# A hybrid layer with a 32-expert MoE: the first expert's up products move into the output-projection stage

## The chip, the cores and the metric

The kernel runs on one core of a Trainium2 chip. The metric is device time in microseconds (us) for one execution. Inputs lie in device memory at the start and the output lies there at the end. The names of the engines are those of the profile: PE is the matrix engine, DVE the vector engine, ACT the scalar engine, POOL the GpSimd engine, and SP the engine that here only issues transfers.

## What is computed

One layer on 2048 tokens of width 1024, in float32: a norm, an input projection, a mixer of 4 mLSTM heads and 4 differential-attention heads, an output projection with a residual, and then the part that matters here, a mixture of experts (MoE) with a residual:

```python
def hierarchical_moe(h, w_group, b_group, w_expert, b_expert, w_gate, w_up, w_down):
    ...
    g_logits = (xt @ w_group).astype(f32) + b_group.astype(f32)
    g_sel = jnp.argmax(g_logits, axis=-1)
    ...
    top_vals, top_idx = lax.top_k(e_in, TOP_K)            # 2 of the 8 experts of one of 4 groups
    eid = (g_sel[:, None] * EXPERTS_PER_GROUP + top_idx).reshape(-1)
    ...
    def expert_block(args):
        xb, e = args
        hid = jax.nn.silu(xb @ w_gate[e]) * (xb @ w_up[e])  # 1024 -> 512, twice
        return hid @ w_down[e]                              # 512 -> 1024
    ...
        h = rms_norm(x, norm2_w[l])
        x = x + hierarchical_moe(h, w_group[l], b_group[l], w_expert[l], b_expert[l],
                                 w_gate[l], w_up[l], w_down[l])
```

So each token goes to two of 32 experts, chosen by its own normalised row, and the experts' token counts depend on the data.

## The kernel before

**Stages.** The input projection and the mixer fill the first half of the span. Then the output projection runs over 16 blocks of 128 tokens (lines 886 to 1162). For each block it multiplies with w_out, adds the residual (`add_half`, line 956), computes the norm's scale (`finish_half`), writes the normalised rows to `h2_d` (`normed`), turns them for the router (`turn_x2`, line 986), computes the router's logits (line 1007 to 1018), and picks experts (`route_a`, `route_b`). `route_b` works out a slot in the table `tb_d` for each token and choice (2048 slots for each expert, filled in token order from `base`), scatters token numbers and weights there by two indirect transfers on POOL's queue (line 1077), and adds to the counts `cnt`. Block i's routing is issued within the loop of block i+1, so only block 15's lies bare at the end.

**Ranking.** After block 15, lines 1136 to 1162 rank the experts by their counts and write `cnti`: which expert stands at which of 32 places, and its count. Experts 0 and 1 are FIXED at places 0 and 1. PE, DVE, ACT and POOL each load their place's count from `cnti` into a register (line 1331) before they go on with a place, and SP loads the expert numbers.

**MoE.** Lines 1163 to 1413 run over the places in an order of instructions written by hand. Each engine runs its instructions in this order. Every weight is split in a high and a low part of a reduced float32 type, and each product takes three matmuls (high by high, low by high, high by low). `ready(u)` splits half a weight tile: the high part on ACT (line 66), the low part on DVE (line 70). Raw weights lie in a ring of 12 slots `R4`, an expert has 6 (4 for gate and up, 2 for down), split tiles lie in a ring of 4, and splits run LOOK = 6 halves ahead of the products. `done(e, j)` reloads a raw slot with the weights of two places on. A place gathers its first 128 tokens' rows from `h2_d` into `xg`, turns them (line 1204), makes 48 up matmuls (`ffn1`, line 1231), the gated hidden layer (`hidden`, lines 1211 to 1213), turns that (`turn_h`, line 1236), and makes 24 down matmuls (`ffn2`, line 1246) one place later, within the next place's turn.

**Later tokens.** If a place has more than 128 tokens, a branch `more{e}` also runs the "few" path: it turns 32 or 64 further rows (line 1265), multiplies them with the raw weights in plain float32 (up at line 1276, down at line 1291), and scatters the result. It reads the same raw slots, which come free for the next weights only behind it.

**The seam** below is the stretch from block 15's routing to the first expert's products. The first six splits stand there, at lines 1319 and 1320, behind the ranking.

## Time and profile before

| what | value |
|---|---|
| median of 3 runs | 2172.4 us (2168.9 to 2178.18) |
| the profiled execution | 2168.61 us, of which the span is 2166.9 us |
| mean granted PE clock in it | 0.981 |
| PE busy | 2048.8 us, 95% of the span |
| DVE, ACT, POOL busy | 1603.8, 1230.9 and 517.1 us |
| projection stage with ranking, about | 1150 to 1378 us |
| MoE, about | 1378 to 2155 us |

The span runs from the first to the last instruction of the profiled execution. The granted clock is a share of full speed, which is 2.4 GHz. A busy share is an average over stages that have different limits, so the rows further down are all from the seam and from the first places of the MoE.

### The profile page before, as it was taken

What the parts mean: (1) busy time and instruction counts of PE and PEld (TensorE: products, weight loads), DVE (VectorE), ACT (ScalarE), POOL (GpSimd) and SP (SyncE); (2) the same over time, 40 slices, a digit from 0 to 9 for tenths busy, and PEclk for the clock granted to TensorE, in tenths of its full rate; (3) what the DMA queues carried; (4) which work ended last, traced back from release to release, by engine and by line L of the source; (5) the groups of instructions that cost most, each with busy time, mean ns of one, the idle gap of its engine ahead of it and who ended that gap; (6) DMA issues with size and microseconds to landing.
All of it is one profiled execution on the core that took longest, in us unless ns stands there. A gap on an engine that the chain in (4) does not pass through costs nothing. (4 is left out here: it accounts for less than half of the span.)

```text
span 2166.9 us, 40488 instructions
## 1 busy us (share of the span) xinstructions
PE 2048.8 (95%) x13815; PEld 1735.3 (80%) x13816; DVE 1603.8 (74%) x4373; ACT 1230.9 (57%) x2820; POOL 517.1 (24%) x685
## 2 busy tenths in 40 slices
PE   7999998999999999999999999599999999999997
PEld 6888887899899999999987888477777666766865
DVE  7667655887788778878886777787887656776863
ACT  5334334666566566656663333477777656667764
POOL 4000004323322332232201111213232332213322
PEclk9999998999999999999999999799999999999999
DMA  7555439645653646375417854499999768898983
GB/s 232 180 171 182 150 111 243 181 123 131 186 152 110 173 149 156 89 195 162 122 51 256 270 145 136 153 328 331 360 344 334 263 218 295 309 317 285 345 285 80
DMA packets 241526, 449.79 MB, mean 208 GB/s; under 512 B 36368, under 2 KB 120400, under 8 KB 231248
## 3 DMA queue, kind: packets, MB, share of 16 engines
q1 hardware_dynamic: 192160, 316.56, 43.3%
q0 software_dynamic: 48800, 128.46, 22.1%
q8 instruction: 161, 2.64, 0.5%
q14 instruction: 133, 1.09, 0.1%
q10 hardware_dynamic: 272, 1.05, 0.1%
HBM read 378.51 MB, written 84.25 MB: 214 GB/s over the span
## 5 line engine op out<-in xcount | busy, mean ns | idle before, releaser
L70 DVE TENSOR_TENSOR L<-R,H 128x1024 fp32r<-128x1024 f32 x408 | 485.9, 1223 | 122.7 <-ACT H L66 119.0
L66 ACT ACTIVATE H<-R 128x1024 fp32r<-128x1024 f32 x408 | 415.8, 1056 | 27.8 <-DVE cnti L1158 9.2
L1231 PE MATMUL pgu<-H,xT 128*128 128x512 f32 x1024 | 360.1, 410 | 14.4 <-issue 5.9
L1231 PEld LDWEIGHTS pgu<-H,xT 128*128 128x128 f32 x1024 | 196.1, 192 | 57.5 <-issue 15.7
L585 ACT ACTIVATE prob<-sc,nm 128x512 f32<-128x512 f32 (+3 forms) x320 | 195.9, 623 | 48.9 <-DVE nm L582 44.0
L574 DVE TENSOR_REDUCE mx<-sc 128x1 f32<-128x512 f32 (+3 forms) x320 | 186.9, 602 | 32.4 <-PE sc L573 16.5
L1231 PE MATMUL pgu<-L,xT 128*128 128x512 f32 x512 | 203.0, 397 | 0.0
L570 PE MATMUL sc<-kt,qt 128*128 128x512 f32 (+3 forms) x640 | 190.2, 387 | 10.1 <-DMA kt<-k_d 7.8
L1246 PE MATMUL py<-H,hT 128*128 128x512 f32 x512 | 177.2, 409 | 11.8 <-issue 10.2
L629 PE MATMUL w<-va,aT 128*128 128x128 f32 x1088 | 155.7, 277 | 6.0 <-ACT raw L510 4.4
L94 PE MATMUL w<-H,hs 128*128 128x256 f32 x512 | 156.6, 306 | 5.0 <-DVE num L690 4.4
L500 PE MATMUL w<-hs,H 128*128 128x256 f32 x512 | 157.8, 308 | 2.0 <-ACT tho L545 0.9
L474 POOL DMA_DIRECT2D qt<-q_d x128 | 77.9, 615 | 296.7 <-DMA q_d<-qkT 274.6
L629 PEld LDWEIGHTS w<-va,aT 128*128 128x128 f32 x1088 | 139.3, 191 | 11.6 <-ACT raw L510 7.3
L95 PE MATMUL w<-L,hs 128*128 128x256 f32 x512 | 145.8, 285 | 0.0
L96 PE MATMUL w<-H,hs 128*128 128x256 f32 x512 | 145.5, 284 | 0.0
L502 PE MATMUL w<-hs,L 128*128 128x256 f32 x512 | 144.8, 283 | 0.0
L501 PE MATMUL w<-hs,H 128*128 128x256 f32 x512 | 144.7, 283 | 0.0
L1246 PEld LDWEIGHTS py<-H,hT 128*128 128x128 f32 x512 | 98.2, 192 | 45.1 <-issue 23.1
L570 PEld LDWEIGHTS sc<-kt,qt 128*128 128x128 f32 x640 | 100.5, 192 | 18.1 <-issue 7.9
L1193 POOL DMA_INDIRECT xg<-h_d,ix x64 | 90.4, 1412 | 97.6 <-PE pt L1204 35.7
L1308 POOL TENSOR_SCALAR yE<-yE,ix 32x1024 f32<-32x1024 f32 (+1 forms) x20 | 57.0, 2852 | 232.0 <-ACT yE L1307 223.9
(374 smaller groups left out, 5227.7 us busy)
## 6 DMA issues: line engine op xcount, KB each, us to landing
R<-w_gate SPq DMA_DIRECT2D x128, 512.0 KB, 10.9
R<-w_up SPq DMA_DIRECT2D x128, 512.0 KB, 11.8
R<-w_down SPq DMA_DIRECT2D x63, 1024.0 KB, 12.7
hs<-hT_d POOLq DMA_DIRECT2D x62, 1024.0 KB, 5.3
hT_d<-hs SPq DMA_DIRECT2D x16, 1024.0 KB, 3.9
qt<-q_d POOLq DMA_DIRECT2D x128, 128.0 KB, 6.4
xt<-x SPq DMA_DIRECT2D x30, 512.0 KB, 4.7
q_d<-qkT SPq DMA_DIRECT2D x32, 256.0 KB, 3.3
```

What stands on the lines that cost most here:

```text
L66: return A.activation(dst, src, AF.Copy, scale=scale)
L70: return V.tensor_tensor(dst, src, h.bitcast(F32), OP.subtract)
L94: T.matmul(ps, xh, wh, start=start, stop=False)
L95: T.matmul(ps, xh, wl, start=False, stop=False)
L96: T.matmul(ps, xl, wh, start=False, stop=stop)
L500: T.matmul(ps, l0, m0, start=d == 0, stop=False)
L570: T.matmul(ps[:, :n], QT[g // 2][:, o, m, g % 2 * P:(g % 2 + 1) * P], KT[r * 4 + c][:, m, :n], start=o == 0, stop=o == 1 and c < sb)
L574: V.reduce_max(B["mx"][:, m, c:c + 1], ps[:, :n], axis=AX.X)
L585: mark["ACT"] = A.activation(B["p", m][:, c2 * 512:c2 * 512 + n], B["sc", m, c2][:, :n], AF.Exp, bias=nm, scale=0.125, accum_out=B["rs"][: ...
L629: T.matmul(po, B["aT", c][:, kb * P:(kb + 1) * P], VA[r * 4 + c][:, kb, :], start=c == 0 and kb == 0, stop=c == nch - 1 and kb == nb[c] - 1)
L1231: T.matmul(pgu[c], xT[:, l, d, :], r[:, :, n], start=d == 0 and m == 0, stop=d == DC - 1 and m == 2)
L1246: T.matmul(py[n], hT[:, l, f, :], r[:, c], start=f == 0 and m == 0, stop=f == 3 and m == 2)
```

## The change

It has three parts. **Early slots.** In block 15's loop, `first_slots` raises `base` and `cnt` of expert 0 to at least 128, so that its tokens of the last two blocks go to slots from 128 on, loads the slots that blocks 0 to 13 filled (`ix0`), and gathers their rows to `xg1`. Expert 0 has 96 tokens with the reference's inputs (worked out from its router); 85 of them are in blocks 0 to 13 and 11 in the last two, so its count becomes 139, and the branch `more0` is taken, which it wasn't. **Early products.** The six first splits, the turn of `xg1` (`first_turn`) and 48 up matmuls (`first_up`) with eight more splits and the gated hidden layer now stand in the projection stage; the last six splits are held behind `posi`, the slots of block 15. In the MoE, place 0 has no up products: it turns `TH`, makes its 24 down matmuls at once, then turns place 1's rows and runs its few path; place 1 has no down products beside its up products. **Room.** For this, four tiles moved to an earlier pool, one weight slot fewer is loaded early (EARLY, 11 to 10), the router's weights lie in a raw slot, and block 15's `normed` runs in one pass on DVE rather than on ACT and POOL.

```diff
-EARLY = 11
+EARLY = 10
...
+        xg1 = wp.tile([P, D], F32, name="xg1")
+        xTs = [wp.tile([P, 2, DC, P], F32R, name="xT0")]
+        TH = [wp.tile([P, 256], F32, name=f"TH{c}") for c in range(2)]
+        ix0 = wp.tile([P, 2, 4], F32, name="ix0")
+
...
-            if e:
-                order_of_use += [6 * (e - 1) + 4, 6 * (e - 1) + 5]
+            if e != 1:
+
+                f = max(e - 1, 0)
+                order_of_use += [6 * f + 4, 6 * f + 5]
 
         def first_half(e):
 
-            return 12 * e - 4 if e else 0
+
+            return 12 * e - 4 if e > 1 else 12 * e
...
                 rows = slice(i * P, (i + 1) * P)
-                CT[i] = sp.tile([P, D], F32, name="ct", bufs=1)
...
-            wr = sp.tile([P, DC, NL], F32, name="wr", bufs=1)
+            wr = R4[9][:, :DC * NL].rearrange("p (c n) -> p c n", c=DC)
...
                 R = RT[i]
-                if i < NB - 1:
-                    V.scalar_tensor_tensor(R["h2"], XT[i], R["ry"], n2b, op0=OP.mult, op1=OP.mult)
-                else:
-                    A.activation(R["h2"], XT[i], AF.Copy, scale=R["ry"])
-                    G.tensor_tensor(R["h2"], R["h2"], n2b, OP.mult)
+                V.scalar_tensor_tensor(R["h2"], XT[i], R["ry"], n2b, op0=OP.mult, op1=OP.mult)
                 nc.sync.dma_start(h2_d[i * P:(i + 1) * P, :], R["h2"])
...
                 posi = sp.tile([P, 2], I32, name="posi")
-                V.tensor_copy(posi, pos)
+                mark["DVE"] = V.tensor_copy(posi, pos)
                 st = [G.indirect_dma_start(out=tb_d, out_offset=bass.IndirectOffsetOnAxis(ap=posi[:, j:j + 1], axis=0),
                                            in_=en[:, j, :], in_offset=None) for j in range(2)]
                 tc.declare_no_dep(st[1].ins, st[0].ins, reason="slots of another expert")
                 V.tensor_tensor(cnt, pr[:, 1, :], cnt, OP.add)
+
+            def first_slots():
+
+                V.tensor_scalar(base[:, 0:1], base[:, 0:1], float(P), None, op0=OP.max)
+                V.tensor_scalar(cnt[:, 0:1], cnt[:, 0:1], float(P), None, op0=OP.max)
+                nc.sync.dma_start(ix0[:, 0], tb_d[0:P, :])
+                G.indirect_dma_start(out=xg1, out_offset=None, in_=h2_d[:S - 2 * P],
+                                     in_offset=bass.IndirectOffsetOnAxis(ap=ix0[:, 0, 0:1].bitcast(I32), axis=0),
+                                     bounds_check=S - 2 * P - 1, oob_is_err=False)
+
+            def first_turn(hf):
+                pt = pp.tile([P, 4, P], F32, name="pt", bufs=2)
+                for j in range(4):
+                    T.transpose(pt[:, j, :], xg1[:, (hf * 4 + j) * P:(hf * 4 + j + 1) * P], ident)
+                h = slice(hf * 4, hf * 4 + 4)
+                split_h(xTs[0][:, 0, h, :], pt)
+                split_l(xTs[0][:, 1, h, :], pt, xTs[0][:, 0, h, :])
+
+            def first_up(pgu, d):
+                wh, wl = (t.rearrange("p (m n) -> p m n", m=2) for t in parts(d // 2, d % 2))
+                for c in range(2):
+                    n = slice(c * 256, (c + 1) * 256)
+                    for m, (l, r) in enumerate(((0, wh), (0, wl), (1, wh))):
+                        T.matmul(pgu[c], xTs[0][:, l, d, :], r[:, :, n], start=d == 0 and m == 0, stop=d == DC - 1 and m == 2)
+
+            def gated(th, pgu, n, behind=None):
+                a1 = A.activation(th, pgu[:, :n], AF.Tanh, scale=0.5)
+                v1 = V.scalar_tensor_tensor(th, th, 1.0, pgu[:, :n], op0=OP.add, op1=OP.mult)
+                if behind:
+
+                    after(a1, behind["ACT"])
+                    after(v1, behind["DVE"])
+                V.tensor_tensor(th, pgu[:, n:2 * n], th, OP.mult)
+                return th
 
             finish_block(0, None)
...
                         route_b(i - 2)
+                    if i == NB - 1 and d == 1:
+                        first_slots()
                     if i + 1 < NB and d in (4, 6):
                         turn_block(i + 1, d // 2 - 2)
...
                 part(d, 1)
+                if d < LOOK:
+                    ready(d)
                 if d == 0:
                     route_b(i - 1)
+                if d in (2, 3):
+                    first_turn(d - 2)
                 if d == 4:
                     turn_x2(i, 0)
...
             route_a(i)
+            route_b(i)
             normed(i)
-            route_b(i)
+            pgu = [pp.tile([P, 512], F32, name=f"pj{n}", bufs=2) for n in range(2)]
+            for d in range(DC):
+                first_up(pgu, d)
+                sl = ready(d + LOOK)
+                if d + LOOK >= DC:
+                    after(sl, mark["DVE"])
+            for c in range(2):
+                gated(TH[c], pgu[c], 256, mark)
...
                 tc.tile_pool(name="pm", bufs=1, space=PSUM, reuse_waits="tile") as pp:
             R4 += [sp.tile([P, 2048], F32, name=f"R{j}", bufs=1) for j in range(EARLY, RAWS)]
             xg0 = sp.tile([P, D], F32, name="xg0", bufs=1)
-            xg1 = sp.tile([P, D], F32, name="xg1", bufs=1)
             yE = sp.tile([P, D], F32, name="yE", bufs=1)
-            for t in (xg0, xg1, yE):
+            xTs.append(sp.tile([P, 2, DC, P], F32R, name="xT1", bufs=1))
+            for t in (xg0, yE):
                 G.memset(t, 0.0)
 
...
                                                 max_val=NE - 1, skip_runtime_bounds_check_because="a place's expert")
+                    if i == 0:
+                        IX[0] = ix0
+                        nc.sync.dma_start(ix0[:, 1], tb_d[P:2 * P, :])
+                        return
 
                     IX[i] = sp.tile([P, 2, 4], F32, name="ix2", bufs=AHEAD + 5)
                     e = eid[i]
...
             why = "counts of 2048 tokens"
-            for i in range(AHEAD):
+            for i in (1, 0, 2):
                 fetch_slots(i)
-            gather(IX[0][:, 0], xg1)
             gather(IX[1][:, 0], xg0)
-            for u in range(LOOK):
-                ready(u)
-            xT = new_xT()
-            turn(xT, xg1)
 
             for t in range(EARLY, RAWS):
                 load_next(t, nc.scalar)
-            py, hT, th, waiting = None, None, None, None
+            xT, py, hT, th, waiting = None, None, None, TH, None
             for e in range(NE + 1):
                 u = first_half(e)
                 fetch_slots(e + AHEAD)
                 if e < NE:
                     n = nc.values_load(cnti[:1, n_at + e:n_at + e + 1], min_val=0, max_val=S, skip_runtime_bounds_check_because=why)
                     gather(IX[e][:, 1], xg1)
-                    xTn = new_xT() if e + 1 < NE else None
-                    pgu = new_pgu()
+                    xTn = new_xT(e + 1) if e + 1 < NE else None
+                    if e:
+                        pgu = new_pgu()
+                    else:
+
+                        hT, py = new_hT(), new_py()
+                        for d in range(2):
+                            turn_h(TH[d], hT, d)
+                        for f in range(4):
+                            ffn2(py, hT, f, parts(4 + f // 2, f % 2))
+                            ready(8 + f + LOOK)
                     for d in range(DC):
-                        ffn1(pgu, xT, d, parts((u + d) // 2, d % 2))
-                        ready(u + d + LOOK)
-                        if d < 2 and e:
+                        if e:
+                            ffn1(pgu, xT, d, parts((u + d) // 2, d % 2))
+                            ready(u + d + LOOK)
+                        if d < 2 and e > 1:
                             if d == 0:
                                 hT = new_hT()
                             turn_h(th[d], hT, d)
...
                             tc.mark_branch_hint_location(f"more{e}", n > P, engines)
-                    thn = [hidden(p, 256) for p in pgu]
+                    thn = [gated(TH[c], pgu[c], 256) for c in range(2)] if e else TH
                 else:
                     emit(*waiting)
                     hT = new_hT()
                     for d in range(2):
                         turn_h(th[d], hT, d)
                     thn = None
-                if e:
+                if e > 1:
...
                 def down(f):
-                    if e:
+                    if e > 1:
                         v = first_half(e) + (8 if e < NE else 0) + f
                         ffn2(py, hT, f, parts(v // 2, v % 2))
...
-                if e:
-                    waiting = (py, IX[e - 1][:, 0])
+                waiting = None if e == 1 else (py, IX[max(e - 1, 0)][:, 0])
                 if e < NE:
                     xT, th = xTn, thn
```

**How the rows stand.** Three places show it. The lists are of DVE's and PE's instructions in program order; `L` and `H` are the split tiles, `R` a raw slot, `TH` the hidden layer of place 0, `pt` and `pj` and `py` PSUM tiles, and + stands for the change, - for before (the line numbers are each kernel's own).

DVE, second half of block 15, one piece of the difference:

```order
+L1080 CAST posi<-pos 128x2
 L70 TENSOR_TENSOR hT<-pt,hT 128x4x128
-L956 TENSOR_TENSOR xt<-pj_17792,xt 128x512
-L978 TENSOR_TENSOR ss<-ss 128x1
+L70 TENSOR_TENSOR L_3616<-R_15365,H_3615 128x1024
+L964 TENSOR_TENSOR xt<-pj_17779,xt 128x512
+L1072 MEMSET en 128x2
+L70 TENSOR_TENSOR L_3618<-R_15366,H_3617 128x1024 x2
+L986 TENSOR_TENSOR ss<-ss 128x1
```

Splits (`L` from `R` and `H`) now stand among block 15's own work, ahead of the residual addition of its second half (L964, before L956) and of the norm's scale.

DVE at the end of the stage, before:

```order
-L1147 TENSOR_SCALAR o_18066<-ident,oc 32x32
-L1154 TENSOR_REDUCE oc<-t_18057 32x1
-L1150 TENSOR_SCALAR o_18066<-prk,oc 32x32
-L1151 TENSOR_REDUCE oc<-o_18066 32x1
-L1152 TENSOR_SCALAR o_18066<-io_15396,oc 32x32
-L1158 CAST cnti<-prk 1x64
-L70 TENSOR_TENSOR L_115<-R_112,H_113 128x1024 x2
-L70 TENSOR_TENSOR L_116<-R_15364,H_114 128x1024 x2
-L70 TENSOR_TENSOR L_3616<-R_15365,H_3615 128x1024 x2
-L70 TENSOR_TENSOR xT<-pt,xT 128x512 x2
```

and in the change:

```order
+L1189 SCALAR_TENSOR_TENSOR t_18147<-cnt,m_15402 32x96
+L1080 CAST posi<-pos 128x2
+L70 TENSOR_TENSOR L_115<-R_15367,H_113 128x1024 x2
+L70 TENSOR_TENSOR L_116<-R_15368,H_114 128x1024 x2
+L70 TENSOR_TENSOR L_3616<-R_15369,H_3615 128x1024 x2
+L1112 SCALAR_TENSOR_TENSOR TH_15375<-TH_15375,pj_18075 128x256
+L1112 SCALAR_TENSOR_TENSOR TH_15376<-TH_15376,pj_18076 128x256
+L1117 TENSOR_TENSOR TH_15375<-pj_18075,TH_15375 128x256
+L1117 TENSOR_TENSOR TH_15376<-pj_18076,TH_15376 128x256
+L1191 TENSOR_REDUCE oc<-t_18147 32x3
```

Six splits and the four gating operations, which were behind the ranking or not there, now stand between `posi` and the rest of the ranking.

PE at the end of the stage and the begin of the MoE, before:

```order
-L1149 MATMUL prk<-o_18066,ones_15410 32x32
-L1156 MATMUL prk<-o_18066,pcol 1x32
-L1157 MATMUL prk<-o_18066,oc 1x32
-L1204 MATMUL pt<-ident,xg_18096 128x128 x8
-L1331 TENSOR_LOAD cnti
-L1231 MATMUL pgu<-H_113,xT 128x512
-L1231 MATMUL pgu<-L_115,xT 128x512
```

and in the change, the same place:

```order
+L1201 MATMUL prk<-o_18156,ones_15412 32x32
+L1208 MATMUL prk<-o_18156,pcol 1x32
+L1209 MATMUL prk<-o_18156,oc 1x32
+L1378 TENSOR_LOAD cnti
+L1288 MATMUL pt<-ident,TH_15375 128x128 x2
+L1288 MATMUL pt<-ident,TH_15376 128x128 x2
+L1298 MATMUL py_18221<-H_113,hT 128x512
+L1298 MATMUL py_18221<-L_115,hT 128x512
```

and, 20 matmuls further on, from the last two down matmuls of place 0 to the first raw up matmuls of its few path:

```order
+L1298 MATMUL py_18222<-L_116,hT 128x512
+L1298 MATMUL py_18222<-H_114,hT 128x512
+L1260 MATMUL pt<-ident,xg_18186 128x128 x4
+L1408 REGISTER_ALU
+L1517 BRANCH_PREFETCH_HINT
+L1260 MATMUL pt<-ident,xg_18186 128x128 x4
+L1427 COMPARE_AND_BRANCH
+L1428 REGISTER_ALU
+L1517 BRANCH_PREFETCH_HINT
+L1317 MATMUL pt<-ident,xg_15373 128x32 x8
+L1328 MATMUL px<-R_112,xH 32x256 x8
```

The up products of place 0 that followed the load of `cnti` are gone from there; behind the load come the hidden layer's turn, the 24 down matmuls, the turn of place 1's rows, a branch, and the few path (L1317, L1328).

## Rows read from the trace of the kernel before

**Rows 1.** The page: each engine's busy time, share of the span, instructions.

```profile
PE 2048.8 (95%) x13815; PEld 1735.3 (80%) x13816; DVE 1603.8 (74%) x4373; ACT 1230.9 (57%) x2820; POOL 517.1 (24%) x685
```

**Rows 2.** Windows of the seam: length, engines' busy time (instructions), PEclk, DMA share, GB/s.

```profile
1353.96:1377.62 23.66, 9.73 (x52) 6.84 (x50) 18.85 (x89) 5.20 (x14) 8.70 (x10) 0.73 0.18 68
...
1385.02:1401.36 16.34, 13.96 (x57) 10.69 (x57) 13.65 (x16) 11.41 (x14) 3.63 (x3) 0.88 0.94 336
...
1386.00:1388.00 2.00, 1.78 (x5) 1.27 (x5) 1.64 (x3) 1.73 (x2) 0.68 (x1) 0.50 1.00 347
...
1401.36:1415.47 14.11, 14.11 (x60) 11.28 (x61) 10.89 (x13) 8.67 (x12) 1.41 (x2) 0.88 0.29 81
...
1402.00:1406.00 4.00, 4.00 (x13) 3.06 (x12) 2.32 (x3) 1.33 (x2) 0.00 (x0) 0.57 0.01 0
```

**Rows 3.** Waits of DVE from 1353.96 to 1377.62: total, times, longest.

```profile
DVE xt L956 <- PE pj L96: 1.3, 1, 1.3
DVE ss L978 <- ACT h L976: 0.8, 1, 0.8
...
DVE hT L70 <- ACT hT L66: 0.5, 1, 0.5
```

**Rows 4.** Timeline of DVE at the seam: start, length, line, operation.

```profile
1368.19 1.48 DVE L1036 CAST sel<-xe 128x2 f32<-128x2 uint32 x1
...
1373.30 0.37 DVE L1147 TENSOR_SCALAR o<-ident,oc 32x32 f32<-32x32 f32 x1
...
1374.55 2.31 DVE L1152 TENSOR_SCALAR o<-io,oc 32x32 f32<-32x32 f32 x1
...
1377.41 0.21 DVE L1158 CAST cnti<-prk 1x64 int32<-1x64 f32 x1 [0.55 <-PE prk L1157]
...
1378.84 6.96 DVE L70 TENSOR_TENSOR L<-R,H 128x1024 fp32r<-128x1024 f32 x6 [1.22 <-ACT H L66]
...
1385.73 1.27 DVE L70 TENSOR_TENSOR xT<-pt,xT 128x512 fp32r<-128x512 f32 x2
...
1416.78 0.41 DVE L1212 SCALAR_TENSOR_TENSOR th<-th,pgu 128x256 f32<-128x256 f32 x1
```

**Rows 5.** Timelines of POOL, SP and PE at the seam.

```profile
1374.97 1.86 POOL L1174 MEMSET xg<- 128x1024 f32 x2
...
1380.24 1.92 POOL L1193 DMA_INDIRECT xg<-h_d,ix  x1 [0.30 <-DVE L L70]
...
1378.35 0.40 SPq L1189 DMA_DIRECT2D ix<-tb_d  x1
...
1383.20 1.94 PE L1204 MATMUL pt<-ident,xg 128*128 128x128 f32 x8 [5.82 <-DMA xg<-h_d,ix]
```

**Rows 6.** Windows of down products, a few path, and an undisturbed expert's up products.

```profile
1415.47:1420.91 5.44, 5.44 (x25) 4.50 (x24) 5.37 (x9) 5.20 (x7) 1.00 (x1) 1.00 0.98 383
...
1451.11:1463.36 12.25, 12.25 (x131) 8.09 (x131) 7.11 (x11) 5.70 (x13) 0.00 (x0) 1.00 0.84 302
...
1463.36:1475.71 12.35, 12.35 (x61) 10.14 (x60) 10.90 (x12) 11.79 (x17) 6.56 (x4) 1.00 1.03 355
```

**Rows 7.** Timelines of PE, ACT and DVE in the first few path.

```profile
1453.31 3.66 PE L1276 MATMUL px<-R,xH 128*32 128x256 f32 x64
...
1458.39 0.27 PE L1282 MATMUL pt<-ident,th 128*128 128x128 f32 x1
...
1459.98 1.93 PE L1291 MATMUL px<-R,hH 128*32 128x256 f32 x32
...
1451.58 0.53 ACT L1267 ACTIVATE xH<-pt 128x128 f32<-128x128 f32 x2
...
1458.70 0.28 ACT L1283 ACTIVATE hH<-pt 128x128 f32<-128x128 f32 x1 [0.34 <-PE pt L1282]
...
1457.66 0.29 DVE L1213 TENSOR_TENSOR th<-px,th 128x128 f32<-128x128 f32 x1
```

**Rows 8.** Waits of PE from 1353 to 1452.

```profile
PE pgu L1231 <- DVE th L1213: 2.2, 1, 2.2
```

More of the change, by code (lines that the diff above doesn't have):

```diff
@@ L874, in split @@
             split_h(hi, raw)
-            split_l(lo, raw, hi)
+            return split_l(lo, raw, hi)
         def ready(u):
             if u < 2 * len(order_of_use):
-                split(order_of_use[u // 2] % RAWS, u // 2, u % 2)
+                return split(order_of_use[u // 2] % RAWS, u // 2, u % 2)
         def done(e, j):
@@ L941, in block_kernel @@
             before = sp.tile([P, P], BF16, name="before", bufs=1)
-            jp = sp.tile([P, P], I32, name="jp", bufs=1)
+            jp = R4[9][:, 512:512 + P].bitcast(I32)
             G.iota(jp, pattern=[[1, P]], base=0, channel_multiplier=-1)
@@ L1195, in gather, with new_xT @@
                                      bounds_check=S - 1, oob_is_err=False)
-            def new_xT():
-                return sp.tile([P, 2, DC, P], F32R, name="xT")
+            def new_xT(i=0):
+                return xTs[i % 2]
             def turn(xT, xg, hfs=(0, 1)):
@@ L1207, in turn, with hidden @@
                     split_l(xT[:, 1, h, :], pt, xT[:, 0, h, :])
-            def hidden(pgu, n):
-                th = sp.tile([P, n], F32, name=f"th{n}", tag=f"th{n}", bufs=3 if n == P else 2)
-                A.activation(th, pgu[:, :n], AF.Tanh, scale=0.5)
-                V.scalar_tensor_tensor(th, th, 1.0, pgu[:, :n], op0=OP.add, op1=OP.mult)
-                V.tensor_tensor(th, pgu[:, n:2 * n], th, OP.mult)
-                return th
+            def hidden(pgu):
+                return gated(sp.tile([P, P], F32, name="th128", bufs=3), pgu, P)
             def new_pgu():
@@ L1277, in few_ffn1 @@
                                  start=d == 0, stop=d == DC - 1, skip_group_check=True)
-                return hidden(px, P)
+                return hidden(px)
             def few_turn_h(th, hH, c):
@@ L1433, in block_kernel @@
                             for c in range(2):
-                                turn_h(hidden(pgu[c], 256), hT, c)
+                                turn_h(gated(TH[c], pgu[c], 256), hT, c)
                             for f in range(4):
```

3 lines of the change are left out of this document (2 added, 1 removed).

## The prediction

> **What bounds the kernel now.** I began with the page: PE is busy for 95% of the span [rows 1], so a change pays only if it takes work from PE or closes one of its gaps. Then the windows. At the seam, from block 15's residual addition at 1353.96 to the end of the cast that writes `cnti` at 1377.62, PE is busy for 9.73 of 23.66 us and DVE for 18.85 [rows 2]; the reader is to see that this stretch is a chain on DVE. Its waits are short: 1.3 for the addition's product, 0.8 for the norm's sum, 0.5 for a turn [rows 3], and 0.55 for the ranking's last matmuls [rows 4]. From the cast on PE still needs 7.40 us (slots, gather, turn [rows 5], a split [rows 4]) to its first up product at 1385.02; the first expert's 48 up products take from there to 1401.36 and the second's 14.11 more, where an undisturbed expert takes 12.35 [rows 2, 6]. So the change takes bare PE time out of this stretch, but hands the splits that go with it to DVE, which bounds the seam.
>
> **Part one: DVE's chain up to `cnti`.** All that the change gives DVE between those two points stands ahead of the cast in program order:
> - 14 splits: six take 6.96, so 1.16 each [rows 4], 16.2;
> - two halves of the first expert's turned rows: 1.27 for two [rows 4], 1.3;
> - `normed`, one pass over a tile of the size of a split, 1.2;
> - four gating operations of 0.41 [rows 4], 1.6;
> - two one-column maxima: nearest are the small operations of 0.2 [rows 4], with their gaps 0.3.
>
> These come to 20.6. Off go 1.3 of the cast at 1368.19, which took 1.48 where the one at 1377.41 takes 0.21, and 1.9 of L1152's 2.31, whose like at 1373.30 takes 0.37 [rows 4]: 3.2. The first long row stands where POOL ran its part of block 15's `normed`, which is gone. The second overlaps POOL's clearing of `xg`, 1374.97 to 1376.83 [rows 5]; in the change that clearing follows block 15's scatters, so falls beside the six late splits.
>
> The Trainium skill, SBUF — State Buffer, section Who interferes with whom, says that DVE and GpSimd share a port pair which one instruction holds to its end: a DVE operation in a two-port mode takes it, or one with two SBUF inputs against a GpSimd operation that reads SBUF. The row of 2.31 agrees. By that rule the clearing, which reads nothing, leaves the splits alone and 1.9 is saved; if it stretched one of them as it stretched L1152, the sum would be 1.9 more. The rule also speaks against the change, as splits have two SBUF inputs and more of POOL's transfers now run beside them.
>
> What that costs is to be seen in a row: of the seam's gathers, the one under the splits took 1.92 on POOL [rows 5], while the six splits beside it kept their 1.16. It falls on transfers, not on DVE's chain.
>
> So far 23.66 + 20.6 - 3.2 = 41.1. DVE's idle 4.8 (23.66 - 18.85) can take up some of it: all of it leaves 36.3, none 41.1. I let the splits fill the waits of rows 3, 2.6, and leave the rest, which belongs to the ranking's matmuls and to gaps between small operations: 38.5. `cnti` is then written at 1392.5, **14.8 later**. The bounds are 12.6 and, with the clearing stretching an operation again, 19.3.
>
> What is hidden: ACT's 14 high parts, since ACT is busy for 5.20 us of the stretch [rows 2] and has no more than 15 to add. PE's 48 products, in the 14 us in which PE has nothing [rows 2]. The wait of `first_turn` for its rows: index load to turn took 4.85 at the seam (1378.35 to 1383.20 [rows 5]), `first_slots` stands some nine steps of three matmuls ahead, 6 us at 0.23 each (24 take 5.44 [rows 6]), but behind block 13's scatters on POOL; PE may wait for up to 2.5, while DVE has eight splits queued, 9.3. If that cover fails, the addition of block 15's second half and all behind it is late by what is left. The second weight slot that is now loaded at the seam serves the second expert's down products, 20 us and more later. The tiles that moved issue the same instructions.
>
> **Part two: PE from `cnti` to place 2.** Before, from the cast's end to 1401.36: 23.7. Now, in PE's order:
> - the load of the count, 0.7, as from the cast to the transfer behind it (1378.35 [rows 5]);
> - the hidden layer's turn: as in the few path 0.6 from its transposes at 1458.39 to the end of ACT's at 1458.98 [rows 7], and DVE's 0.4: 1.0;
> - 24 down matmuls, 5.4 [rows 6], and 1.8 for a PE that has stood still: the first expert's window is 4.0 longer than 12.35, of which 2.2 is a wait [rows 2, 6, 8], and from 1386 to 1388 the granted clock is 0.50, the lower of its two levels, 1.2 GHz [rows 2]: 7.2;
> - eight transposes of the second expert's rows: 1.94 at the lower clock [rows 5], so 1.0;
> - the few path for the 11 tokens. The window of 12.25 has 24 down matmuls in it, so it costs 6.8 there [rows 6]. Here no product covers its waits: 1.0 for the rows' turn (1451.11 to ACT's end at 1452.11), 3.7 up, 1.0 to the end of the gating at 1457.95, 0.6 turn, 1.9 down [rows 6, 7]: 8.2. Bounds 6.8, and 10.0 with a clock dip as above.
>
> Sum 18.2, or 5.6 less; place 1's first up product comes at 1410.7. Its window was 14.1, and 5.4 of down products followed [rows 2, 6]. Now it has no down products and no turn of a hidden layer (four transposes, 0.3): 12.05, with up to 1.5 for a PE that the few path's waits left at the lower clock. Then place 2 waits for place 1's gating, 2.2, as place 1 did where nothing stood between [rows 8], and runs slow behind that wait by 1.8, as 14.11 against 12.35. 17.5 for 19.5: 2.1 less.
>
> **Sum.** 14.8 - 5.6 - 2.1 = **+7.2**, rounded terms. The profiled time of 2168.6 becomes 2175.8; the median lies 3.8 above that execution, so 2179.6 there, 0.3% more. From then on place follows place as before. With DVE's chain at 12.6 or 19.3, the few path at 6.8 or 10.0, and the dip of place 1 at 0 or 1.5, it's +2.1 to +13.5, or 2174 to 2186.
>
> **Rivals.**
>
> *PE stays at the lower clock (slower).* It stands still at `cnti`, twice in the few path, and behind place 1. After the wait of 2.2 the granted clock was 0.57 from 1402 to 1406 [rows 2]. If it is 0.50 from the hidden layer's turn through the few path, the down products cost 10.9, not 7.2, and the few path's 5.6 of matmuls double: +16, 2189. Against it stands a clock of 1.00 in the first few path [rows 6], though there down products filled the waits. It decides once place 1 starts after 1415.
>
> *Weights come late (slower).* The few path reads four raw slots to 1407, so the load of place 2's weights, which was under way by 1386 at 347 GB/s [rows 2], starts only then. Four slots of 1.05 MB take 12 us, and half of the 4.85 for two transfers in a row to land: 1421.5. Place 2 starts at 1426.4 and splits its fourth slot just then, so 5 us are to spare. From 1402 to 1406 the queue stood at 0.01 while PE worked [rows 2], so there was slack. Each us beyond is a us; the whole shift of the load, 21, would make +16 more than the spare allows, but half of it is likelier: +15, 2187.
>
> *The few path isn't taken (same).* If the late tokens don't bring the count past 128, its 8.2 and the dip of 1.5 go: -2.5, 2170. The 11 tokens speak against it.
>
> *DVE hides more (faster).* If only what stands behind `posi` counted, six splits and the gating, 8.6 - 3.2 = 5.4, the sum is -2.3, and without the few path -12: 2160. But 4.8 of idle can't hold 12 more us of splits, and the order is fixed.
>
> **How the numbers follow.** My forecast gets 0.62, the lower clock 0.20, late weights 0.07, the few path untaken 0.08, hidden splits 0.03. I call 0.5%, 10.9 us, no change: a measurement of this kernel can hardly tell less, as its three runs span 9.3. Faster than that is only the last case with some scatter: 0.04. Slower, above 2183, are the lower clock and late weights most of the time, 0.24, and a sixth of the forecast's own cases, 0.10: 0.34. Within are the other 0.62. The range goes from 2171, near the untaken path, to 2190, which takes in the lower clock.
>
> **What the profile after would show.** The cast into `cnti` ends at about 1392 (1390 to 1397); from 1354 on DVE is busy for 36 us or more with hardly a wait, and the ranking's L1204 (L1152 before) is short. PE then stands at the load of `cnti`; 24 down matmuls follow, the first at clock 0.5, then a few path of 8 us with its waits, and place 1 near 1411. Place 2 comes 7 us later than before, and this shift stays to the end. I would be wrong if `cnti` came before 1388, if the clock stayed low through the few path, or if place 2 waited for a load, so that the shift grew after 1426.

## The result and the profile after

The changed kernel takes 2185.37 us (median of 8 runs, 2181.19 to 2187.44) against 2174.35 us before (8 runs, 2168.90 to 2178.18). The ratio is 1.0053 with a 95% interval of 1.0037 to 1.0068, so the change costs 8 to 15 us, 11 as the medians have it. The forecast was 7.2 more, 2179.6 from the 2172.4 of the three runs then known, with 2171 to 2190.

The profiled execution took 2183.06 us with a span of 2181.3. Its windows are laid as those of before [rows 2, 6], from block 15's first residual addition on: the seam up to the cast into `cnti`, from there to place 1, the 24 down matmuls and the raw up products in that, then place 1, and place 2 up to its first down product (length, busy time by engine, PEclk, DMA share, GB/s).

```profile
1352.12:1393.73 41.61, 22.24 (x108) 17.27 (x106) 36.22 (x110) 19.08 (x31) 14.23 (x9) 0.81 0.13 47
1393.73:1416.55 22.82, 18.62 (x142) 12.36 (x142) 7.43 (x11) 6.86 (x12) 3.07 (x3) 0.75 0.44 154
1396.07:1404.32 8.25, 8.25 (x25) 6.48 (x26) 5.55 (x6) 4.23 (x5) 0.74 (x1) 0.66 0.82 306
1407.47:1412.82 5.35, 5.35 (x66) 2.64 (x64) 0.00 (x0) 0.28 (x1) 0.00 (x0) 0.68 0.27 86
1416.55:1431.40 14.85, 12.32 (x60) 9.75 (x57) 11.63 (x13) 13.16 (x19) 7.23 (x4) 1.00 1.02 361
1431.40:1448.02 16.62, 14.46 (x61) 11.07 (x61) 11.35 (x14) 9.12 (x13) 3.94 (x4) 0.90 1.05 364
```

The first stretch is 41.61 us where it was 23.66, so 18.0 longer rather than 14.8. The second is 22.8, forecast 18.2: its down matmuls took 8.25 at a granted clock of 0.66, and the raw up products 5.35 at 0.68, where they took 3.66 before [rows 7]. Place 1 is the one shorter than forecast, 14.85 rather than 15.7, at full clock throughout.

What DVE waits for in the first stretch, the largest two (total, times, longest):

```profile
DVE at L1074 <- PE prk L1064: 2.4, 1, 2.4
DVE xT L70 <- ACT xT L66: 1.0, 1, 1.0
```

And DVE's timeline there, from the addition to the cast:

```profile
1352.12 0.69 DVE L964 TENSOR_TENSOR xt<-pj,xt 128x512 f32<-128x512 f32 x1
...
1379.80 6.88 DVE L70 TENSOR_TENSOR L<-R,H 128x1024 fp32r<-128x1024 f32 x6
...
1388.19 2.50 DVE L1213 CAST cnti<-cnt 1x32 int32<-1x32 f32 x1
...
1392.74 0.23 DVE L1204 TENSOR_SCALAR o<-io,oc 32x32 f32<-32x32 f32 x1
...
1393.52 0.21 DVE L1210 CAST cnti<-prk 1x64 int32<-1x64 f32 x1 [0.55 <-PE prk L1209]
```

The six late splits run back to back. Behind them a cast of 32 numbers takes 2.50 us, while the ranking's L1204 (L1152 before, 2.31 [rows 4]) is down to 0.23. POOL's timeline names what stood beside it:

```profile
1380.64 6.89 POOL L1081 DMA_INDIRECT tb_d<-en,posi  x1 [9.97 <-DVE posi L1080]
...
1388.80 0.96 POOL L1226 MEMSET xg<- 128x1024 f32 x1
```

Block 15's first scatter takes 6.89 us, just the time of the six splits, so that the clearing of `xg`, 1374.97 before [rows 5], comes at 1388.80, on the ranking. PE's timeline over the same stretch and behind it:

```profile
1359.50 1.06 PE L1098 MATMUL pt<-ident,xg 128*128 128x128 f32 x8 [2.75 <-DMA xg<-h_d,ix]
...
1394.32 1.09 PE L1288 MATMUL pt<-ident,TH 128*128 128x128 f32 x4 [0.83 <-DVE cnti L1210]
...
1396.07 0.79 PE L1298 MATMUL py<-H,hT 128*128 128x512 f32 x1 [0.66 <-ACT hT L66]
...
1404.32 1.03 PE L1260 MATMUL pt<-ident,xg 128*128 128x128 f32 x8
1406.50 0.40 PE L1317 MATMUL pt<-ident,xg 32*128 32x32 f32 x4 [1.15 <-issue]
```

```profile
1413.96 0.30 PE L1334 MATMUL pt<-ident,th 128*128 128x128 f32 x1 [1.14 <-DVEq L1432]
...
1431.40 0.47 PE L1283 MATMUL pgu<-H,xT 128*128 128x512 f32 x1 [2.53 <-DVE TH L1117]
...
1441.13 0.63 PE L1260 MATMUL pt<-ident,xg 128*128 128x128 f32 x4 [1.85 <-DMA xg<-h_d,ix]
```

PE waits 2.75 us for the early gather; behind `cnti` stand the turn, the 24 down matmuls, the eight transposes, and then waits of 1.15, 0.24 (left out here) and 1.14 in the few path. Place 2 starts 2.53 behind place 1's last product, as place 1 did before [rows 8], and loses 1.85 more on the rows of place 3.

The first down product behind place 2's up products, before and then in the change, closes this part:

```profile
1433.25 0.39 PE L1246 MATMUL py<-H,hT 128*128 128x512 f32 x1
```

```profile
1448.02 0.47 PE L1298 MATMUL py<-H,hT 128*128 128x512 f32 x1 [0.30 <-ACT TH L1111]
```

Up to there the changed kernel needs 95.90 us from the addition (1448.02 - 1352.12); before it was 79.29 (1433.25 - 1353.96). So 16.6 us are lost in the seam and the two places behind it, more than the 11 by which the kernel became slower.

### The profile page after: what moved, and what is told of

Same layout as the page of the kernel before. It is cut to its first block, busy times and chain, and to the rows that moved or that the text cites. A ratio compares the mean times of both kernels' runs of the same rounds, so it can differ in the third digit from the quotient of the medians.

```text
span 2181.3 us, 40744 instructions
## 1 busy us (share of the span) xinstructions
PE 2060.8 (94%) x13920; PEld 1736.8 (80%) x13921; DVE 1605.1 (74%) x4378; ACT 1233.3 (57%) x2827; POOL 519.5 (24%) x685
## 5 line engine op out<-in xcount | busy, mean ns | idle before, releaser
L1283 PE MATMUL pgu<-H,xT 128*128 128x512 f32 x992 | 346.6, 407 | 10.6 <-ACT H L66 4.3
L1283 PEld LDWEIGHTS pgu<-H,xT 128*128 128x128 f32 x992 | 188.3, 190 | 53.4 <-issue 7.9
L1283 PE MATMUL pgu<-L,xT 128*128 128x512 f32 x496 | 195.9, 395 | 0.3 <-issue 0.3
L1298 PEld LDWEIGHTS py<-H,hT 128*128 128x128 f32 x512 | 98.6, 193 | 41.2 <-issue 16.1
L1307 POOL DMA_INDIRECT out<-y,ix x32 | 57.8, 1806 | 221.5 <-ACT y L1303 96.4
## 6 DMA issues: line engine op xcount, KB each, us to landing
R<-w_up SPq DMA_DIRECT2D x128, 512.0 KB, 12.2
```

What stands on the lines that cost most here:

```text
L1283: T.matmul(pgu[c], xT[:, l, d, :], r[:, :, n], start=d == 0 and m == 0, stop=d == DC - 1 and m == 2)
L1298: T.matmul(py[n], hT[:, l, f, :], r[:, c], start=f == 0 and m == 0, stop=f == 3 and m == 2)
```

## The experiments

All runs are read from block 15's first residual addition, because the stages ahead of it scatter. The table shows differences of starts in each run's own trace: the end of the cast into `cnti` after the addition, place 1's first up product after the cast, the hidden layer (tanh) of place 4 and the end of the span after the addition, and the timed ratio to before. Each is one profiled execution.

| run | cast | place 1 | place 4 | end | ratio (95% interval) |
|---|---|---|---|---|---|
| before | 23.7 | 23.7 | 121.6 | 812.9 | |
| before, again | 24.1 | 25.4 | 123.9 | 812.9 | |
| changed | 41.6 | 22.8 | 138.6 | 829.2 | 1.0053 (1.0037 to 1.0068) |
| changed, again | 42.7 | 22.1 | 140.0 | 824.8 | |
| DVE halves behind the ranking | 34.4 | 25.1 | 134.7 | 829.8 | 1.0056 (1.0037 to 1.0074) |
| slots of blocks 0 to 12 | 38.1 | 22.1 | 135.4 | 823.7 | 1.0032 (1.0019 to 1.0045) |
| clearing on ACT | 40.7 | 22.2 | 138.2 | 826.8 | 1.0037 (1.0023 to 1.0051) |
| no few path at place 0 | 44.2 | 17.3 | 134.6 | 821.0 | 1.0040 (1.0024 to 1.0055) |
| the same, early hint | 44.1 | 12.2 | 127.8 | 814.3 | 0.9990 (0.9973 to 1.0008) |
| three repairs | 35.8 | 22.0 | 133.1 | 821.8 | 1.0018 (1.0004 to 1.0031) |
| three repairs, downs in the few path | 35.8 | 27.4 | 136.7 | 845.3 | 1.0132 (1.0107 to 1.0157) |
| three repairs, DVE halves behind | 29.1 | 25.4 | 128.5 | 819.2 | 1.0035 (1.0020 to 1.0050) |
| three repairs, downs in the ranking | 38.0 | 21.4 | 130.8 | 823.0 | 1.0021 (1.0006 to 1.0036) |
| three repairs, no few path at place 0 | 35.8 | 12.2 | 119.7 | 803.3 | 0.9967 (0.9954 to 0.9979) |

**Both kernels profiled again.** No edit.

> A second profiled execution of the kernel before, unchanged. If a profiled execution stands for the kernel, the start of block 15's first residual addition is at 1354 within 1 us, the cast into cnti ends 23.7 us later, and the time from place 4's hidden layer to the end is 691 us within 2. Rival: the mixer ahead of the seam, or the MoE's waits for issue, differ from execution to execution by several us, so that the 14.4 us between the two profiled spans hold some us that are not the change's.

> A second profiled execution of the changed kernel, unchanged. The seam's own lengths (cast into cnti 41.6 us after the addition, place 1's first up product 22.8 us behind it) return within 1 us if they are the kernel's; the addition's start (1352 in the first) shows how far the stages ahead of it scatter; from place 4's hidden layer to the end 691 us in the first.

The addition and the cast of the kernel before, again:

```profile
1361.98 0.69 DVE L956 TENSOR_TENSOR xt<-pj,xt 128x512 f32<-128x512 f32 x1
...
1385.89 0.21 DVE L1158 CAST cnti<-prk 1x64 int32<-1x64 f32 x1 [0.55 <-PE prk L1157]
```

and of the changed kernel:

```profile
1359.21 0.69 DVE L964 TENSOR_TENSOR xt<-pj,xt 128x512 f32<-128x512 f32 x1
...
1401.71 0.21 DVE L1210 CAST cnti<-prk 1x64 int32<-1x64 f32 x1 [0.55 <-PE prk L1209]
```

The addition started at 1361.98 and 1359.21, where it was 1353.96 and 1352.12: the same code ahead of it scatters by 7 to 8 us. The cast returns within 1.1 us of its distance, place 1 within 1.7. From the addition to the end, before took 812.9 twice, the change 829.2 and 824.8, so 12 to 16 us more; the 14.4 between the two spans shown first happen to lie in it. The rival was right, and every further comparison starts at the addition. From place 4 to the end the changed kernel took 690.6 and 684.8 us, so differences below some 6 us in the column of ends say little.

Behind place 4 the distance between the two kernels doesn't stay the same. Counted from the addition, the changed kernel's tanh comes 17.0 us later at place 4, 25.3 at place 9, 9.1 at place 29 and 15.7 at place 31; in the second pair of executions it is 16.1, 22.2, 5.0 and 12.2. Two of these steps are waits of PE for nothing that the trace shows, in the few path of place 8 in the changed kernel and in that of place 20 before:

```profile
1585.14 0.50 PE L1298 MATMUL py<-H,hT 128*128 128x512 f32 x1 [4.03 <-issue]
```

```profile
1874.40 0.80 PE L1246 MATMUL py<-H,hT 128*128 128x512 f32 x1 [4.20 <-issue]
```

Both return in the second execution of their kernel (4.23 and 3.96). Why the two kernels have them at different places, no run here settles.

**The DVE halves of the last six early splits behind the ranking** (`high` and `low` make a split's ACT half and its DVE half).

```diff
...
-                sl = ready(d + LOOK)
-                if d + LOOK >= DC:
-                    after(sl, mark["DVE"])
+                if d + LOOK < DC:
+                    ready(d + LOOK)
+                else:
+                    high(d + LOOK)
...
                         hT, py = new_hT(), new_py()
+                        low(DC)
                         for d in range(2):
                             turn_h(TH[d], hT, d)
+                        for w in range(DC + 1, DC + LOOK):
+                            low(w)
```

> The DVE halves of the last six early splits stand behind the ranking again (their ACT halves stay early), one ahead of the hidden layer's turn and five behind it. Theory A (what DVE does ahead of the cast into cnti is the price): cnti comes 6.9 us sooner after block 15's residual addition, 34.7 us rather than 41.6, the 24 down matmuls keep their 8.3 us since DVE makes a half in 1.16 and PE needs 2.1 for its matmuls at first, and the kernel is 6 to 7 us faster than the changed one, about 2178. With the splits away block 15's first scatter on POOL should take 1 to 2 us, not 6.9. Rival B (the splits' time only moves from ahead of the cast to behind it, where PE now waits for them): cnti 6.9 sooner but place 1 less than 2 sooner, and the time within 2 us of the changed kernel's.

The cast comes 7.2 us sooner, as theory A has it, 2.2 of it are lost between the cast and place 1, and place 4 is 3.9 sooner. POOL's scatter, freed from the splits, takes 0.97:

```profile
1385.76 0.97 POOL L1088 DMA_INDIRECT tb_d<-en,posi  x1 [9.76 <-DVE TH L1119]
```

But the time didn't fall (1.0056 for 1.0053). ACT's waits in the MoE are what stands out, here and, in the second row, in the changed kernel:

```profile
ACT H L66 <- issue: 25.9, 5, 5.3
```

```profile
ACT H L66 <- issue: 2.3, 2, 1.2
```

Five times ACT stands for about 5 us ahead of a split, with nothing in the trace that it waits for, five places apart each time (places 7, 12, 17, 22 and 27). At four of the five, the next place's tanh follows this one's after 19.9 to 20.1 us, where the changed kernel has 18.0 to 18.6: 6.7 us in all, enough to take back the 3.9. So theory A holds for the seam, the time is rival B's but not for its reason, and neither theory foresaw what the build does to the MoE.

**Slots read a block sooner.**

```diff
-                    if i == NB - 1 and d == 1:
+                    if i == NB - 1 and d == 0:
                         first_slots()
...
-                                     bounds_check=S - 2 * P - 1, oob_is_err=False)
+                                     bounds_check=S - 3 * P - 1, oob_is_err=False)
```

(and the call stands ahead of block 13's `route_b`).

> The first expert's early slots are read one block sooner (tokens of blocks 0 to 12; 27 tokens go late, which is still one group of 32), so the gather of its rows is under way some 14 us before first_turn. Theory A (in the changed kernel PE's 2.75 us wait for that gather went on to DVE, as idle of 1.0 and 2.4 us ahead of the cast): cnti comes 2 to 3.4 us sooner after the addition, the time 2 to 3 us lower than the changed kernel's, about 2182. Rival B (as predicted, DVE's queued splits cover that wait, and its idle is for something else): cnti and time unchanged.

The two waits of DVE are gone from this trace (the longest left is 0.5), and the cast ends 38.06 after the addition, 3.6 sooner:

```profile
1359.71 0.69 DVE L964 TENSOR_TENSOR xt<-pj,xt 128x512 f32<-128x512 f32 x1
...
1397.56 0.21 DVE L1210 CAST cnti<-prk 1x64 int32<-1x64 f32 x1 [0.55 <-PE prk L1209]
```

Theory A: the wait for the gather went on to DVE's chain. In time that is some 5 us (1.0032 for 1.0053), with nearly as much uncertainty. The six traces that read the slots as the changed kernel does have these two waits, 3.4 to 5.9 us in sum, and in the five others that read them sooner they are gone as well. Take them off, and the casts of the changed kernel's two executions and of the first two runs without the few path, 41.6 to 44.2 in the table, come to 38.0 to 38.3, which is this run's 38.1.

**Clearing on ACT.**

```diff
             for t in (xg0, yE):
-                G.memset(t, 0.0)
+                A.activation(t, R4[0][:, :D], AF.Copy, scale=0.0)
```

> xg and yE are cleared by ACT (a copy scaled by zero) rather than by POOL. Theory A (POOL's clearing, late by the long scatter, stretched the ranking's small operations at 1388 from 0.2 to 2.5 us): the three long operations are 0.2 us each, cnti comes 2.2 us sooner, and the time is 2 us lower than the changed kernel's. Rival B (it was the scatter on POOL, or something else on DVE, that stretched them): the long operations stay, the time is the same within 1 us.

The cast of 32 numbers is back at 0.16:

```profile
1393.21 0.16 DVE L1213 CAST cnti<-cnt 1x32 int32<-1x32 f32 x1
```

though the scatter is as long as before:

```profile
1385.67 6.88 POOL L1081 DMA_INDIRECT tb_d<-en,posi  x1 [9.74 <-DVE posi L1080]
```

So it was the clearing that stretched the ranking, as theory A says. The cast into `cnti` is only 0.9 sooner, as DVE's waits for the gather were 1.5 longer in this execution (4.9 rather than 3.4); next to the changed kernel's second execution, where they were 4.7, it is 2.0 sooner. In time it is 3.5 us (1.0037), within the uncertainty.

**Place 0 without its few path** (11 late tokens left out), and then with the branch's hint behind the load of the count:

```diff
-                    n = nc.values_load(cnti[:1, n_at + e:n_at + e + 1], ...
+                    n = nc.values_load(cnti[:1, n_at + e + (e == 0):n_at + e + (e == 0) + 1], ...
...
+                        tc.mark_branch_hint_location(f"more{e}", n > P, engines)
                         hT, py = new_hT(), new_py()
...
```

(the hint is an instruction ahead of a branch that is given the branch's condition).

> Place 0 reads place 1's count, so its few path isn't run and the first expert's 11 late tokens are left out of the result. Theory A (the path costs PE the 10 us that the trace shows, with a wait of 1.2 for its first transposes, and holds back the weights of place 2 and with them the gather of place 3's rows): 11 to 14 us faster than the changed kernel, 2171 to 2174, as before the change; the weights of place 2 are asked for some 15 us sooner. Rival B (the predicted price): 8 us faster. Rival C (the stream of weights, not PE, sets the pace of the next places): less than 5 us faster.

> As the run without place 0's few path (the first expert's 11 late tokens are left out), but the hint for its branch is given right behind the load of the count, some 9 us ahead of the branch, not just ahead of it. Theory A (PE's 5.7 us at the branch in that run was the wait for the other path's instructions, so the few path's price was hidden by it): place 1's first up product comes about 11.5 us after the cast into cnti rather than 17.3, and the time is 5 us lower than without the early hint, about 2177. Rival B (PE there waited for place 1's weights or rows): no difference.

Without the early hint place 1 starts here:

```profile
1420.87 0.77 PE L1283 MATMUL pgu<-H,xT 128*128 128x512 f32 x1 [5.70 <-PEq L1427]
```

and with it here:

```profile
1413.47 0.48 PE L1283 MATMUL pgu<-H,xT 128*128 128x512 f32 x1 [0.57 <-ACT xT L66]
```

In the first run PE waited 5.70 us at its own branch, so taking the path away brought 5.5 us between the cast and place 1, not 10, and some 3 in time: rival C's number, but not its reason. With the hint ahead of the down matmuls that wait is gone (the 0.57 left is for place 1's turned rows), so theory A holds for the hint, with some 11 us in time rather than 5; place 1 comes 12.2 us after the cast, and the kernel is as fast as before the change. The few path therefore costs 10 us between cast and place 1 (22.1 and 22.8 against 12.2), and in time 1.0053 to 0.9990, 14 us with some 5 of uncertainty.

**Three repairs with the whole computation**: sooner slots, clearing on ACT, early hint (27 late tokens, still one group).

> Three repairs of the changed kernel together, with the whole computation: slots read a block sooner, clearing on ACT, and place 0's branch hint behind the load of the count. Theory A (the three costs stand one behind the other on the chain): cnti 6 us sooner after the addition than in the changed kernel (35.6 us), the few path begins 1 us sooner, and the time is 6 to 8 us below the changed kernel's, 2178, still 3 us above before. Rival B (the seam isn't what sets the end): the cast comes sooner but the time stays above 2182.

The cast is 5.8 us sooner, and the ratio 1.0018: 7 to 8 us of the 11 are regained, with some 5 of uncertainty, as theory A has it. The early hint brought nothing on the path that is taken: the 1.15 us at the few path's first transposes stayed.

```profile
1404.42 0.40 PE L1317 MATMUL pt<-ident,xg 32*128 32x32 f32 x4 [1.15 <-issue]
```

**Down matmuls within the few path.**

```diff
-                        for f in range(4):
-                            ffn2(py, hT, f, parts(4 + f // 2, f % 2))
-                            ready(8 + f + LOOK)
...
                 def down(f):
+                    if e == 0:
+                        ffn2(py, hT, f, parts(4 + f // 2, f % 2))
+                        ready(8 + f + LOOK)
```

> The three repairs, and place 0's 24 down matmuls are no longer made ahead of its few path but between its parts, as other places have them. Theory A (the few path is dear because no product covers its waits and the clock falls in it: 10 us here, 6.8 where down matmuls lie between): place 1's first up product 18 to 19 us after the cast into cnti rather than 22, the raw up products take 3.7 us rather than 5.2, and the time is 3 us below the run with three repairs, 2177. Rival B (the path's price is its own matmuls and branches): the same within 1 us.

A miss: the kernel loses 25 us to the run with three repairs. With the down matmuls behind the turn of place 1's rows, nothing covers their gather:

```profile
1405.85 1.94 PE L1260 MATMUL pt<-ident,xg 128*128 128x128 f32 x8 [7.86 <-DMA xg<-h_d,ix]
...
1409.83 0.80 PE L1298 MATMUL py<-H,hT 128*128 128x512 f32 x1
```

PE waited 7.86 us for it, and place 1 came 5.5 later. The rest, 20 us, is lost behind place 4, where ACT again stood for 28 us with nothing that it waits for. These waits don't account for it: the next run has 26 us of them and takes only 2 longer than the three repairs behind place 4 (690.7 for 688.7). What does, and why some builds have such waits, no run here settles.

**Three repairs and the DVE halves behind the ranking.**

> The three repairs, and the DVE halves of the last six early splits behind the ranking. In the earlier run with these halves behind the ranking, place 1 came 5 us sooner but the kernel was no faster, since ACT stood five times for 5 us each in the MoE with no releaser in the trace (26 us of waits for issue; 2.3 in the changed kernel). Theory A (those waits belong to that build's instructions and not to the place of the splits): in this build place 1 comes 5 us sooner than with three repairs alone, and the time is 4 to 5 us lower, 2175. Rival B (they follow from DVE's order): waits for issue of 20 us or more on ACT return, and the time is that of the three repairs, 2180 or above.

Place 4 is 4.6 us sooner than with three repairs alone, and at the end 2.6 are left in this execution and none in the timed runs. ACT's waits for issue are 26.2 us again, at the same places, so they come back with this order of splits: rival B, though the build with down matmuls in the few path has them without it, so that the order of splits is not shown to be their cause.

```profile
ACT H L66 <- issue: 26.2, 5, 5.4
```

**Down matmuls within the ranking** (place 0's rows held in float32r until the scatter).

```diff
+            hT = flat[:, :D].rearrange("p (l f n) -> p l f n", l=2, f=4)
...
             V.tensor_copy(cnti[:, n_max:], mc)
+            py = [pp.tile([P, 512], F32, name=f"pj{n}", bufs=2) for n in range(2)]
+            for f in range(4):
+                wh, wl = parts(4 + f // 2, f % 2)
...
```

> The three repairs, and place 0's hidden layer is turned and its 24 down matmuls are made within the ranking, in the 10 us for which PE waits for DVE there, rather than behind the load of the count; its rows are held in a float32r tile until they are scattered. Theory A (behind cnti, PE has to do only what needs the count): place 1's first up product 12 to 14 us after the cast into cnti rather than 22, cnti itself up to 3 us later as its matmuls stand among the others; the time is 6 to 9 us below the three repairs, 2171 to 2174, level with before or a little faster. Rival B (the few path's own waits and clock take what the downs leave): less than 4 us below.

Rival B. PE's timeline:

```profile
1389.08 1.08 PE L1193 MATMUL pt<-ident,TH 128*128 128x128 f32 x4 [9.02 <-DVE TH L1117]
...
1405.97 1.25 PE L1338 MATMUL pt<-ident,xg 32*128 32x32 f32 x8 [3.32 <-DVE xT L70]
1407.15 5.48 PE L1349 MATMUL px<-R,xH 128*32 128x256 f32 x64
```

The hidden layer comes late from DVE (PE waited 9.02 for it), so the down matmuls still lie partly behind the ranking, the cast is 2.2 later, and the few path waits 3.32 for DVE and runs its raw up products at 5.48 us. Place 1 is no sooner than with the three repairs.

**Three repairs and no few path at place 0** (27 late tokens left out).

> The three repairs, and place 0's few path left out (the first expert's 27 late tokens are missing from the result). Theory A (the change loses in the seam by costs that add up: the few path 10 us, gather wait and clearing 6 us): place 1's first up product 50 us after block 15's residual addition, where before the change it was 47.4 and in the changed kernel 64.4, and since the place's down products then no longer follow, the time is 7 us below the run without the few path and with the early hint, 2168, which would be 6 us faster than before. Rival B (the MoE behind takes back what the seam gives, as it did with the late splits): 2172 or more, no faster than before.

Place 1 starts right behind the down matmuls and the transposes:

```profile
1394.26 0.80 PE L1298 MATMUL py<-H,hT 128*128 128x512 f32 x1 [0.37 <-ACT hT L66]
...
1404.11 0.47 PE L1283 MATMUL pgu<-H,xT 128*128 128x512 f32 x1 [0.56 <-ACT xT L66]
```

That is 48.0 us after the addition where it was 47.4 before, with place 0's down products already made. The ratio is 0.9967: theory A, 7 us faster than before. With the three repairs the few path thus costs 11 us in time (1.0018 to 0.9967) and 9.8 between cast and place 1. Of the builds here, only this one, without the late tokens, is faster than before.

## Why the prediction came out as it did

The kernel became slower by the way forecast: more delay in `cnti` than the products taken off PE are worth, and a few path on top. The time came out in the range, 11 us later rather than 7.2, but that it is so near is in part luck. The sum of +7.2 was for the seam and two places, with bounds of +2.1 and +13.5, and there the change lost 16.6: 18.0 up to the cast for 14.8, 0.9 won back up to place 1 for 5.6, and 0.4 by place 2's down products for 2.1. The MoE behind, where nothing was forecast, gave 0.8 and 4.2 us of it back in the two pairs of executions; where the rest of the way to 11 lies, two pairs can't tell. The forecast also called up to 10.9 us no change, with a chance of 0.62, and more than that slower, with 0.34; 11, with an interval of 8 to 15, lies on the line between the two. By its steps:

- **DVE's chain up to `cnti`: 18.0, forecast 14.8, bounds 12.6 to 19.3.** The sum of work came out, 36.2 us busy for 36.3, by errors that cancel: 2.3 of it are the stretched cast, so the rest was less than summed, though no one row shows where (six splits took 6.88 for 6.96). The idle was wrong: 5.4 us, where 2.2 were to remain.
- **"while DVE has eight splits queued", failed.** DVE ran its instructions in program order, and behind its first four splits stand the first half of the turned rows and `at` of block 14's routing, which waits for a small matmul that PE has behind `first_turn`. The wait for the gather therefore stopped DVE for 1.0 and 2.4 us; with the slots read a block sooner both are gone and 3.6 us come back. What counts of a queue is the first instruction that waits, not how much work lies in it.
- **"It falls on transfers, not on DVE's chain", failed.** I had POOL's transfers slower by 0.9 under splits, from the row of a gather; the scatter took 6.89 beside six of them and 0.97 with these moved away. Late by that, the clearing fell not on the splits but on the ranking, and stretched its cast by 2.3, where the upper bound had 1.9 and the forecast nothing; with the clearing on ACT the cast is back at 0.16. The Trainium skill's SBUF — State Buffer, section Who interferes with whom, says that a DVE operation with two SBUF inputs contends with a GpSimd operation that reads SBUF. These runs agree, with 6.89 and 0.97; but the section doesn't say for how long a run of such operations holds a scatter, and it reports a probe in which `tensor_tensor` did not stall a transfer, so it would not have given the size.
- **From the cast to place 1: 22.8, forecast 18.2.** The load and the turn 2.3 for 1.7, the down matmuls 8.25 for 7.2, the transposes with the wait behind them 2.2 for 1.0, the few path 10.05 for 8.2 (its upper bound was 10.0). The lower clock, which I had as a rival for the whole stretch, is part of it: 0.66 and 0.68 granted in its two long pieces.
- **Place 1's dip of 1.5 didn't come**, at a granted clock of 1.00. Place 2's wait and slow start did, 2.53 for 2.2.
- **Late weights.** Place 2's weights were asked for at 1414, 62 us after the addition, and splits had them in time but for 0.7. Instead place 3's gather came 1.9 late, beside a DMA share of 1.05; the rival with 5 us to spare was near its edge.
- **"From then on place follows place as before", failed by place, and nearly came out in the sum.** The two pairs of executions were 17.0 and 16.1 us apart at place 4, 25.3 and 22.2 at place 9, 9.1 and 5.0 at place 29, and 16.2 and 11.9 at the end. PE's waits for nothing that the trace shows fall on other places in the two kernels; their cause stays open.

The dearest piece is the few path: 10 us by the run without it, 8.2 forecast. Without it and with the early hint the change is level with before (0.9990), and with the three repairs it pays (0.9967).

## What to carry to other kernels

Moving work ahead of a point that everything waits for pays only if the engine in front of that point has room: here PE had 14 us of idle time, and DVE, which makes PE's operands, under 5. Follow a wait through the program order of each engine that comes behind it, and ask what a transfer that starts late will stand beside. A shortcut that needs a repair path for the few cases it misses has to carry that path's price, here 10 us for 11 tokens, at the one place where nothing covers it.

## What the runs showed of the hardware

POOL's indirect scatter took 0.97 us alone and 6.89 us beside six back-to-back subtractions of two SBUF tiles on DVE, though a gather beside six such subtractions took only 1.92 [rows 4, 5]; what makes the difference, no run here shows. Two clearings on POOL, 0.96 us each, stretched a DVE cast of 32 numbers from 0.16 to 2.50 us. A branch whose hint stands just ahead of it cost PE 5.70 us on the path that isn't the fall-through, and with the hint some 10 us ahead no wait is left there. In the MoE, ACT's waits ahead of splits for nothing that the trace shows come to 26 to 28 us in three builds, in pieces of 5 us five places apart, and to 2.3 to 6.5 us in the other eleven traces (2.3 in both executions of each of the two kernels profiled twice). In the run with the DVE halves behind the ranking, four of the five pieces lengthened a place by 1.5 to 2.1 us; their cause stays open. Block 15's first addition starts between 1352 and 1362 us in the fourteen traces, so that a median of several runs is needed for the time, where a trace can show a stretch to 1 or 2 us.
